# Two-layer trunk on one core: five blocks per MLP with four Strassen groups, twelve raw tiles, the norm scale applied at the down projection

## The chip, the cores and the metric

The kernel runs on one core of a Trainium2 chip. The metric is the device time of one execution in microseconds (us), lower is better. TensorE (PE) multiplies matrices, VectorE (DVE) and ScalarE (ACT) work elementwise, GpSimd (POOL) hardly takes part, and SyncE (SP) issues the transfers of the weights.

## What is computed

256 tokens of 2048 channels pass through two layers: a mixer, then an MLP with a squared ReLU, both behind an RMS norm and added to the residual stream. The change touches the two MLPs and, by the order of work, the pooling mixer of layer 1 that stands between them.

```python
D_FF = 4 * D_MODEL                       # 8192

def rms_norm(x, g):
    y = xf * lax.rsqrt(jnp.mean(xf * xf, axis=-1, keepdims=True) + EPS)
    return y * g

def multiscale_pool(h, w, b, scale):     # group i: trailing mean over WINDOWS[i] minus the token
    ...
    y = jnp.einsum('btgc,gcd->btgd', d, w).reshape(bsz, t, D_MODEL) + b
    return y * scale

def sq_relu_mlp(h, w_up, w_down):
    u = jax.nn.relu(h @ w_up)
    return (u * u) @ w_down

for layer in range(DEPTH):               # layer 0: hybrid mixer, layer 1: multiscale_pool
    x = x + mix
    x = x + sq_relu_mlp(rms_norm(x, mlp_norm[layer]), mlp_w_up[layer], mlp_w_down[layer])
```

The norm's factor r of a token can be taken out of the MLP: (relu(r·h W))² = r² (relu(h W))², since r is positive.

## The kernel before

**Precision.** Each fp32 operand is split in two parts: hi, a rounded copy (ACT, L235), and lo, the rest (DVE, L236: raw − hi). A product is made of three matmuls, hi·hi, hi·lo and lo·hi.

**Steps.** All weights are streamed in 846 *steps*, mostly of 512 KB. SP issues the load of a step into a *raw* tile (L206), ACT and DVE split it into a hi and a lo tile (L235, L236), PE multiplies. There are 7 raw tiles and 4 tiles each of hi and lo, used in turn; a load waits until its raw tile's last reader, the lo of seven steps before, is done. Loads are written 9 steps ahead of their matmuls (`AHEAD_LOAD`), splits 3 (`AHEAD_SPLIT`).

**Units.** Steps belong to units of one kind each. *up*: 256 columns of w_up over 16 k-tiles (a k-tile is 128 rows), in a transposed form, with pairs of a 512-wide (L963) and a 256-wide (L965) matmul. *down*: 512 columns of w_down, two k-tiles and 12 matmuls a step (L971), evacuated into the residual `x_sb` by L834; the last chunk of the kernel is cut into two units of 256 columns. *Strassen group*: 1024 columns of w_up in a form of Strassen's algorithm, with fewer products; 12 *sa* steps and 16 *sb* steps of 6 matmuls each (L734). The sb steps come in pairs, and before a pair is split, DVE replaces its two raw tiles by differences in place (L222 to L225). When a group is done, `gen_s` combines the results, squares them and transposes them into the block data.

**Blocks.** The 8192 inner channels of an MLP are taken in 4 blocks of 2048: first the block's up units, then its down units, which multiply the block's 16 k-tiles of u² by 512 columns of w_down at a time, in 8 steps for each of 4 chunks. Block 0 consists of 8 up units; blocks 1 to 3 of 4 up units and one Strassen group. The steps of the next block's Strassen group are held back and let in between the down steps of the block before, as `due()` says: the 12 sa steps beside the first 10 or so of the 32 down steps, then the 8 pairs of sb steps.

**Norm.** The factor r of the norm is spread to a row by a small matmul (`spread`, L317) and multiplied in at the up units' evacuation (L874) and in `gen_s`.

**Pool.** With the first MLP's last down units, `finish` loads the pool's data into slots whose old contents have been read: the pool matrix into slot 6 (L843, copied to slot 7 by ACT in L845), bias into slot 4 and scale into slot 5 (L850). DVE multiplies bias by scale (L854) and adds the product to the residual (`add_bias`, L765). Slots 4 to 7 held the last block's u², k-tiles 0 to 3, 4 to 7 and so on. The pool units' results are split (L863 on ACT, L864 on DVE), multiplied by window matrices (L776 to L780) and added to the residual.

**Order.** The program is written step by step; generators (`lane`) put the other work between the steps. A scheduler then orders each engine's instructions; SP and DVE work their queues in that order.

Of the kernel before, what the change touches and what calls it, by code (L numbers as in the profile page):

```python
# [16 lines left out]
P = 128  # L17
# [5 lines left out]
DFF = 8192  # L23
FB = 2048
NB = DFF // FB
WINS = (2, 4, 8, 16)
# [14 lines left out]
X_EARLY = ((0, 14), (1, 2), (1, 6), (1, 10))  # L41
RAWS, AHEAD_LOAD = 7, 9
WARM = 2
# [4 lines left out]
def plan():  # L48
# [9 lines left out]

    def unit(w, r0, nk, c0, n, kind, arg, src, k0=0, turned=False):
        units.append(dict(w=w, r0=r0, nk=nk, c0=c0, n=n, kind=kind, arg=arg, src=src, k0=k0,  # L60
                          turned=turned))

# [13 lines left out]
    for layer in range(2):  # L76
        if layer == 1:
            for g in range(4):
                unit("pool_w", 512 * g, 4, 0, 512, "pool", g, "pool", 4 * g)
        for b in range(NB):  # L80
            for i in range(8 if b == 0 else 4):
                unit("w_up", D * layer, KT, b * FB + 256 * i, 256, "up", (layer, b, i),
                     f"mlp{layer}", turned=True)
            if b + 1 < NB:
                for kind in ("sa", "sb"):
                    unit("w_up", D * layer, KT, (b + 1) * FB + FB // 2, 512, kind,
                         (layer, b + 1), f"mlp{layer}")
# [12 lines left out]
    for u, d in enumerate(units):  # L100
        c0, n = d["c0"], d["n"]
        if d["kind"] == "sa":
            tiles = [t for k in range(0, KT, 2) for t in ((k, c0), (k + 1, c0), (k + 1, c0 + n))]
            held += [[(u, j, tiles[j : j + 2])] for j in range(0, len(tiles), 2)]
            at = 0
        elif d["kind"] == "sb":
            for k in range(0, KT, 2):
                held.append([(u, 2 * k, [(k, c0), (k, c0 + n)]),
                             (u, 2 * k + 2, [(k + 1, c0 + n), (k + 1, c0)])])
        else:  # L110
            ks = list(range(0, d["nk"], 4 if d["turned"] else 2))
            if u == 0:
                ks = [0, 1, 2, 3] + ks[2:]
            for j, (k, e) in enumerate(zip(ks, ks[1:] + [d["nk"]])):
                seq.append((u, k, [(kk, c0) for kk in range(k, e)]))
                if d["kind"] == "down":
                    at += 1
                    while held and at >= due(20 - len(held)):
                        seq += held.pop(0)
    assert not held  # L120
    steps, off = [], 0
    for u, k, tiles in seq:
        steps.append((u, k, tiles, off))
        off += len(tiles) * P * units[u]["n"]
    return units, steps


@with_exitstack
def tile_trunk(ctx: ExitStack, tc: tile.TileContext, x_in, xt_in, w_all, prm_in,
# [21 lines left out]
    def t4(n, dt=F32):  # L151
        return new("t4", [P, 1036], dt, bufs=5)[:, :n]

# [28 lines left out]
    def load_x(q):  # L182

        m, c = q // 2, slice(D // 2 * (q % 2), D // 2 * (q % 2) + D // 2)
        if q == 0:
# [7 lines left out]
               "u0": u_blk[0], "u1": u_blk[1]}  # L193
    units, steps = plan()
    raws, splits = {}, {}
    done = {"load": 0, "split": 0}

    def load(i):
        u, k, tiles, off = steps[i]
        n, nk = units[u]["n"], len(tiles)  # L200
        raw = v3(new("raw", [P, 1024], bufs=RAWS)[:, : nk * n], nk, n)
        if u == 0:
# [123 lines left out]

    def row2(name):
        return rs[name, "row"][:, None, :].to_broadcast([P, 2, T])

    def norm_chunk(name, c, tiles, slot0, gain):  # L330
# [19 lines left out]

# [328 lines left out]
    def gen_u(b, i, ea, eb, base):  # L679
        yield  # L680
        act.activation(eb, ea, AF.Square)
        if i % 2 == 0:
# [110 lines left out]
    def finish(u, ps):  # L793
# [36 lines left out]
        elif kind in ("out", "down"):  # L830
            c = arg if kind == "out" else arg[2]
            cs = slice(d["c0"], d["c0"] + d["n"])
            for m in range(MT):
                dve.tensor_tensor(x_sb[m][:, cs], x_sb[m][:, cs], ps[:, m, : d["n"]], ALU.add)  # L834
# [32 lines left out]
        elif kind == "up":  # L867
            layer, b, i = arg
            name = f"mlp{layer}"
            need(lambda: (name, "row") in rs)  # L870
            e = ev()
            ea, eb = v3(e[:, 0], 2, T), v3(e[:, 1], 2, T)
            add_halves(ea, ps)
            dve.scalar_tensor_tensor(ea, ea, 0.0, row2(name), ALU.max, ALU.mult)  # L874
            lane.append(gen_u(b, i, ea, eb, u_base(layer, b)))
# [53 lines left out]
    for i, (u, k, tiles, _) in enumerate(steps):  # L929
# [118 lines left out]
```

## Time and profile before

| | us |
|---|---|
| three runs: median (lowest to highest) | 2166.05 (2165.43 to 2166.27) |
| profiled execution, its own time | 2164.82 |
| its span | 2163.0 |
| ACT busy | 1203.2 |
| DVE busy with lo (L236), 846 instructions | 1012.2 |
| DVE busy with the sb operations (L222 to L225), 48 of each | 132.2 |

Rows of the timeline give the start in us, the duration in us, engine, line, operation, output<-inputs, and in brackets the idle time before it with what ended it. Busy times of PE are modelled at a matmul's end, so consecutive matmuls overlap and the distance of their starts tells more. A wait in the list of waits names who waited, for whom, the sum in us, how many times, and the longest.

### The profile page before, as it was taken

To read this page: it belongs to the slowest core of one execution; us is meant where nothing else is said; L and a number is where in the kernel's file an instruction comes from. 1 tells how busy PE (TensorE), PEld (TensorE's weight loads), DVE (VectorE), ACT (ScalarE), POOL (GpSimd) and SP (SyncE) were. 2 spreads that over 40 slices of the span, in tenths; PEclk is the share of its full clock that TensorE was granted. 3 is DMA by queue.
4 is the path that set the end of the run, shared out by engine and by line. 5 is a ranking of instruction groups with operands and counts; after the bars stand their busy time and mean duration, and the time that the engine had idled before them with its cause. 6 is when DMAs were issued, how large, how long until landed. Compare 5 with 4: busy or idle time off the path is not lost.

```text
span 2163.0 us, 28389 instructions
## 1 busy us (share of the span) xinstructions
PE 2154.4 (100%) x10613; PEld 1820.6 (84%) x10613; DVE 1541.7 (71%) x1908; ACT 1203.2 (56%) x1401; POOL 21.7 (1%) x21
## 2 busy tenths in 40 slices
PE   9999999999999999999999999999999999999999
PEld 8888888888888888888888888878888888888888
DVE  6988766656545586876886886578778678678754
ACT  7665456665644465555555555456555555555543
POOL 0000000000000000000000000000000000000000
PEclk9999999999999999999999999999999999999999
DMA  9665455555665567777776776565677677677663
GB/s 334 204 204 166 159 184 166 175 166 166 207 192 191 170 197 240 245 232 215 248 247 202 246 253 186 187 224 162 197 257 250 194 245 243 214 247 238 224 204 117
DMA packets 129002, 454.32 MB, mean 210 GB/s; under 512 B 14496, under 2 KB 17248, under 8 KB 128608
## 3 DMA queue, kind: packets, MB, share of 16 engines
q1 hardware_dynamic: 128000, 451.36, 64.4%
q8 instruction: 83, 1.36, 0.3%
q10 hardware_dynamic: 864, 1.15, 0.2%
q14 instruction: 55, 0.45, 0.1%
HBM read 450.32 MB, written 2.13 MB: 209 GB/s over the span
## 4 chain that ended last, share of the span: by engine, by line
PE 97%; DVE 1%; DMA 1%; issue 0%; ACT 0%; SPq 0%; DVEq 0%; ACTq 0%
PE acc L971 58%; PE acc L963 16%; PE bg L734 10%; PE acc L965 9%; PE bg L294 1%; PE bg L522 1%; DVE lo L236 0%; DMA raw<-w_all 0%; PE bg L579 0%; PE bg L669 0%; PE bg L614 0%; DMA st<-prow_in 0%; DVE st L765 0%; PE bg L610 0%; PE bg L671 0%
## 5 line engine op out<-in xcount | busy, mean ns | idle before, releaser
L235 ACT ACTIVATE hi<-raw 128x1024 fp32r<-128x1024 f32 (+2 forms) x846 | 887.6, 1049 | 889.8 <-PE acc L971 586.2
L236 DVE TENSOR_TENSOR lo<-raw,hi 128x1024 fp32r<-128x1024 f32 (+2 forms) x846 | 1012.2, 1206 | 454.7 <-ACT hi L235 432.4
L971 PE MATMUL acc<-hi,st 128*128 128x512 f32 (+2 forms) x3840 | 1165.6, 386 | 0.9 <-ACT hi L235 0.9
L971 PEld LDWEIGHTS acc<-hi,st 128*128 128x128 f32 x3840 | 710.9, 188 | 142.1 <-ACT hi L235 2.4
L971 PE MATMUL acc<-lo,st 128*128 128x512 f32 (+2 forms) x1920 | 736.2, 385 | 0.4 <-DVE lo L236 0.3
L963 PE MATMUL acc<-st,hi 128*128 128x512 f32 x1568 | 552.4, 394 | 0.0
L965 PE MATMUL acc<-st,lo 128*128 128x256 f32 x1568 | 441.8, 282 | 0.0
L971 PEld LDWEIGHTS acc<-lo,st 128*128 128x128 f32 x1920 | 360.6, 188 | 74.1 <-DVE lo L236 2.2
L963 PEld LDWEIGHTS acc<-st,hi 128*128 128x128 f32 x1568 | 294.3, 188 | 62.1 <-issue 1.4
L965 PEld LDWEIGHTS acc<-st,lo 128*128 128x128 f32 x1568 | 296.3, 189 | 2.0 <-issue 1.4
L734 PE MATMUL bg<-hi,st 128*128 128x512 f32 x672 | 206.9, 389 | 0.0
L734 PEld LDWEIGHTS bg<-hi,st 128*128 128x128 f32 x672 | 126.1, 188 | 26.3
L734 PE MATMUL bg<-lo,st 128*128 128x512 f32 x336 | 130.7, 389 | 0.0
L734 PEld LDWEIGHTS bg<-lo,st 128*128 128x128 f32 x336 | 63.1, 188 | 13.0
L834 DVE TENSOR_TENSOR st<-st,acc 128x512 f32<-128x512 f32 (+1 forms) x74 | 46.4, 669 | 15.9 <-PE acc L971 15.6
L222 DVE TENSOR_TENSOR raw<-raw 128x512 f32<-128x512 f32 x48 | 33.1, 689 | 31.1 <-DMA raw<-w_all 31.0
L223 DVE TENSOR_TENSOR raw<-raw,raw 128x512 f32<-128x512 f32 x48 | 33.1, 690 | 20.7 <-DMA raw<-w_all 19.9
L282 ACT ACTIVATE st<-bg,prm 128x256 fp32r<-128x256 f32 x64 | 28.4, 467 | 22.5 <-DVE st L283 20.9
L325 DVE TENSOR_TENSOR ev<-acc,ev 128x512 f32<-128x512 f32 x40 | 27.4, 686 | 11.6 <-ACT ev L324 11.6
L283 DVE SCALAR_TENSOR_TENSOR st<-bg,prm,st 128x256 fp32r<-128x256 f32 x64 | 29.5, 481 | 8.2 <-ACT st L282 8.2
L225 DVE TENSOR_TENSOR raw<-raw 128x512 f32<-128x512 f32 x48 | 33.1, 690 | 1.0
L224 DVE TENSOR_TENSOR raw<-raw,raw 128x512 f32<-128x512 f32 x48 | 32.9, 686 | 0.2
(187 smaller groups left out, 949.7 us busy)
## 6 DMA issues: line engine op xcount, KB each, us to landing
raw<-w_all SPq DMA_DIRECT2D x818, 512.0 KB, 3.8
raw<-w_all SPq DMA_DIRECT2D x20, 256.0 KB, 2.8
st<-x_in SPq DMA_DIRECT2D x8, 512.0 KB, 7.8
st<-scr SPq DMA_DIRECT2D x8, 512.0 KB, 6.1
raw<-w_all SPq DMA_DIRECT2D x8, 288.0 KB, 8.1
st<-prow_in SPq DMA_DIRECT2D x2, 1024.0 KB, 6.3
st<-xt_in SPq DMA_DIRECT2D x6, 256.0 KB, 7.4
st<-pmat_in SPq DMA_DIRECT2D x1, 768.0 KB, 6.2
```

The lines of the kernel that those rows point to most:

```text
L222: dve.tensor_tensor(raw[:, 0], raw[:, 1], raw[:, 0], ALU.subtract)
L223: dve.tensor_tensor(raw[:, 1], two[:, 0], raw[:, 1], ALU.subtract)
L224: dve.tensor_tensor(two[:, 0], two[:, 0], raw[:, 0], ALU.subtract)
L225: dve.tensor_tensor(two[:, 1], two[:, 0], two[:, 1], ALU.subtract)
L235: act.activation(hi, raw, AF.Copy)
L236: dve.tensor_tensor(lo, raw, hi.bitcast(F32), ALU.subtract)
L283: dve.scalar_tensor_tensor(dst[:, 1, c], ps, gain, dst[:, 0, c].bitcast(F32), ALU.mult, ALU.subtract)
L734: pe.matmul(sps[q], st[h], w[:, j], start=p == 0 and w is hi and h == 0, stop=p == KT // 2 - 1 and w is lo)
L834: dve.tensor_tensor(x_sb[m][:, cs], x_sb[m][:, cs], ps[:, m, : d["n"]], ALU.add)
L963: pe.matmul(ps[:, f].rearrange("p (h t) -> p h t", h=2), hi[:, kk, fs], t[:, :, c], start=first, stop=False)
L965: pe.matmul(ps[:, f, :T], lo[:, kk, fs], t[:, 0, c], start=False, stop=last)
L971: pe.matmul(ps[:, m, :n], t[:, h % 2, c, m * P : (m + 1) * P], (hi, hi, lo)[h][:, kk], start=first and h == 0, stop=last and h == 2)
```

## The change

Each MLP is cut into five blocks: 2048 columns in 8 up units, then four blocks of 1536, each of 2 up units (512 columns) and a Strassen group (1024). So a layer has four Strassen groups instead of three. Down units of blocks 1 to 4 have 12 k-tiles and 6 steps per chunk; their k-tiles are taken in the order 4 to 11, then 0 to 3, which puts the Strassen group's first. `due()` is scaled to the number of down steps.

Outside the mixers, loads may also go to the 5 tiles of the scratch ring `t4`, in a fixed alternation with the 7 raw tiles (`homes`): twelve raw tiles there. `AHEAD_LOAD` is 14.

r is no longer spread to a row for the MLPs. The up results get a plain ReLU on ACT and the square; r² (a column per token half) is multiplied in where a down unit is evacuated, now a SCALAR_TENSOR_TENSOR (x + r²·y).

Lines shift: lo is L270, hi L269, the sb operations L256 to L259, the load L240, the down evacuation L875, bias times scale L895, `add_bias` L800, the pool matmuls' split L904 and L905, the loads of prow L891 and of pmat L884, `put_hi_lo` L318 (L283 before).

```diff
-FB = 2048
-NB = DFF // FB
+SW = 1024
+BLOCKS = ((2048, 0), (512, SW), (512, SW), (512, SW), (512, SW))
+NB = len(BLOCKS)
+BASE = [sum(map(sum, BLOCKS[:b])) for b in range(NB)]
...
-RAWS, AHEAD_LOAD = 7, 9
+RAWS, SPARE, AHEAD_LOAD = 7, 5, 14
...
-            for i in range(8 if b == 0 else 4):
+            for i in range(BLOCKS[b][0] // 256):
...
-                    unit("w_down", DFF * layer + b * FB, KT, c0, n, "down", (layer, b, c),
-                         f"u{b % 2}")
-
-    def due(i):
-        return 1 + 10 * i // 12 if i < 12 else 13 + 19 * (i - 12) // 8
+                    unit("w_down", DFF * layer + BASE[b], sum(BLOCKS[b]) // P, c0, n, "down",
+                         (layer, b, c),
+                         f"u{b % 2}",
+                         own=BLOCKS[b][0] // P if b else 0)
+
+    def due(i, n):
+        a = 5 * n // 16
+        return 1 + a * i // 12 if i < 12 else a + 3 + (n - a - 3) * (i - 12) // 8
...
+        kts = [*range(own, nk), *range(own)]
...
+def homes(units, steps):
+    def free(d):
+        if d["kind"] not in ("up", "sa", "sb", "down"):
+            return False
+        layer, b = d["arg"][:2]
+        return not ((layer, b) == (0, NB - 1) and d["kind"] == "down"
+                    or (layer, b) == (1, 0) and d["kind"] == "up" and d["arg"][2] < 6)
+
+    rings, at, res = {"raw": [], "t4": []}, 0, []
+    size = {"raw": RAWS, "t4": SPARE}
+    for i, (u, *_) in enumerate(steps):
+        ring = "raw"
+        if free(units[u]):
+            at = (at + 1) % (RAWS + SPARE)
+            ring = "t4" if at * SPARE % (RAWS + SPARE) < SPARE else "raw"
+        r = rings[ring]
+        res.append((ring, r[-size[ring]] if len(r) >= size[ring] else -1))
+        r.append(i)
+    return res
...
-        while done["load"] < min(len(steps), i + 1 + AHEAD_LOAD):
+        while (done["load"] < min(len(steps), i + 1 + AHEAD_LOAD)
+               and home[done["load"]][1] < done["split"]):
...
+            if name != "pool":
+                rs[name, "sq"] = new("rsq", [P, MT], bufs=2)
+                dve.tensor_tensor(rs[name, "sq"], r, r, ALU.mult)
...
-        if c == 3 and name != "pool":
-            yield from spread(name)
...
+        act.activation(ea, ea, AF.Relu)
         act.activation(eb, ea, AF.Square)
...
-        act.activation(a[:, 0:2], a[:, 0:2], AF.Relu, scale=r[:, 0:1])
+        act.activation(a[:, 0:2], a[:, 0:2], AF.Relu)
...
-                dve.tensor_tensor(x_sb[m][:, cs], x_sb[m][:, cs], ps[:, m, : d["n"]], ALU.add)
+                o, y = x_sb[m][:, cs], ps[:, m, : d["n"]]
+                if kind == "out":
+                    dve.tensor_tensor(o, o, y, ALU.add)
+                else:
+                    dve.scalar_tensor_tensor(o, y, r2[:, m : m + 1], o, ALU.mult, ALU.add)
...
-            dve.scalar_tensor_tensor(ea, ea, 0.0, row2(name), ALU.max, ALU.mult)
```

**DVE, in the sb steps beside block 0's down units.** The rows are the instructions of DVE's queue, output<-inputs. Names are tiles with running numbers; a raw or t4 tile is written by a load, and the one that takes its buffer over is the seventh raw tile after it before the change, and after it the seventh raw or the fifth t4 tile. Before, `raw_1487` takes over the buffer of `raw_1465`, which `lo_1486` reads last:

```order
L236 TENSOR_TENSOR lo_1486_8670<-raw_1465_8568,hi_1485_8669 128x1024
L224 TENSOR_TENSOR raw_1477_8629<-raw_1477_8629,raw_1474_8611 128x512
L225 TENSOR_TENSOR raw_1477_8629<-raw_1477_8629 128x512
L236 TENSOR_TENSOR lo_1489_8688<-raw_1468_8580,hi_1488_8687 128x1024
L222 TENSOR_TENSOR raw_1487_8685<-raw_1487_8685 128x512
```

After, `t4_1284` takes over the buffer of `t4_1244`, which `lo_1283` reads last:

```order
L270 TENSOR_TENSOR lo_1283_7497<-t4_1244_7313,hi_1282_7496 128x1024
L270 TENSOR_TENSOR lo_1286_7515<-raw_1249_7327,hi_1285_7514 128x1024
L256 TENSOR_TENSOR t4_1284_7512<-t4_1284_7512 128x512
L270 TENSOR_TENSOR lo_1289_7533<-raw_1254_7345,hi_1288_7532 128x1024
L270 TENSOR_TENSOR lo_1292_7549<-t4_1257_7363,hi_1291_7548 128x1024
L257 TENSOR_TENSOR t4_1284_7512<-raw_1287_7530,t4_1284_7512 128x512
L270 TENSOR_TENSOR lo_1295_7561<-raw_1260_7381,hi_1294_7560 128x1024
L258 TENSOR_TENSOR raw_1287_7530<-raw_1287_7530,t4_1284_7512 128x512
L259 TENSOR_TENSOR raw_1287_7530<-raw_1287_7530 128x512
```

Before, a lo and two sb operations stand between the lo that frees the buffer and the first operation on its new tile; here, after the change, one lo.

**DVE, from the first MLP's last down unit to the pool units.** Before (`st4` and `st5` are bias and scale, `st12` and `st13` the residual, `acc_72` the last down unit's result):

```order
L236 TENSOR_TENSOR lo_2016_11720<-raw_1992_11582,hi_2015_11719 128x1024
L854 TENSOR_TENSOR st4_1936_11251<-st4_1936_11251,st5_1937_11252 128x512
L854 TENSOR_TENSOR st4_1936_11251<-st4_1936_11251,st5_1937_11252 128x512 x3
L765 TENSOR_TENSOR st12_849_4939<-st12_849_4939,st4_1936_11251 128x512
...
L236 TENSOR_TENSOR lo_2019_11738<-raw_1995_11602,hi_2018_11737 128x1024
L236 TENSOR_TENSOR lo_2022_11756<-raw_1999_11624,hi_2021_11755 128x1024
L834 TENSOR_TENSOR st12_849_4939<-st12_849_4939,acc_72_11608 128x512
L834 TENSOR_TENSOR st13_850_4940<-st13_850_4940,acc_72_11608 128x512
```

After (`acc_74` is the last down unit's result, `acc_75` the first pool unit's):

```order
L875 SCALAR_TENSOR_TENSOR st13_850_4940<-acc_74_11684,rsq_1044_6082,st13_850_4940 128x512
L270 TENSOR_TENSOR lo_2068_11816<-raw_2044_11678,hi_2067_11815 128x1024
L270 TENSOR_TENSOR lo_2078_11863<-raw_2048_11700,hi_2077_11862 128x1024
L372 TENSOR_REDUCE sum_2070_11835<-ss_2002_11426 128x2
...
L895 TENSOR_TENSOR st4_1997_11399<-st4_1997_11399,st5_1998_11400 128x512
L895 TENSOR_TENSOR st4_1997_11399<-st4_1997_11399,st5_1998_11400 128x512 x3
L800 TENSOR_TENSOR st12_849_4939<-st12_849_4939,st4_1997_11399 128x512
...
L905 SCALAR_TENSOR_TENSOR t4_2080_11881<-acc_75_11819,rstd_2071_11837,t4_2079_11880 128x512
L270 TENSOR_TENSOR lo_2083_11889<-raw_2051_11718,hi_2082_11888 128x1024
```

The multiplication of bias by scale and the six additions that follow stood ahead of the last down unit's evacuation; they now stand behind it, and ahead of the first pool unit's L905.

**SP, at the same place.** Before:

```order
L206 DMA raw_2002_11642<-w_all 128x1024
L850 DMA st4_1936_11251<-prow_in 128x2048
L206 DMA raw_2007_11670<-w_all 128x1024
L206 DMA raw_2011_11697<-w_all 128x1024
L850 DMA st5_1937_11252<-prow_in 128x2048
L206 DMA raw_2014_11717<-w_all 128x1024
L843 DMA st6_1933_11245<-pmat_in 128x1536
```

After:

```order
L891 DMA st5_1998_11400<-prow_in 128x2048
L240 DMA raw_2056_11746<-w_all 128x1024
L240 DMA raw_2060_11773<-w_all 128x1024
L884 DMA st6_1994_11393<-pmat_in 128x1536
L240 DMA raw_2063_11793<-w_all 128x1024
L240 DMA raw_2066_11813<-w_all 128x1024
L891 DMA st4_1997_11399<-prow_in 128x2048
```

The load of the bias into slot 4 was the first of the three and is now the last; slot 4's old contents, the k-tiles 0 to 3 of the last block, are read last.

More of the change, by code (lines that the diff above doesn't have):

```diff
@@ L57, in plan, with unit @@
     units = []
-    def unit(w, r0, nk, c0, n, kind, arg, src, k0=0, turned=False):
+    def unit(w, r0, nk, c0, n, kind, arg, src, k0=0, turned=False, own=0):
+        kts = [*range(own, nk), *range(own)]
         units.append(dict(w=w, r0=r0, nk=nk, c0=c0, n=n, kind=kind, arg=arg, src=src, k0=k0,
-                          turned=turned))
+                          turned=turned, kts=kts))
     unit("w_in", 0, KT, CB, 512, "b", None, "h")
@@ L80, in plan @@
         for b in range(NB):
-            for i in range(8 if b == 0 else 4):
-                unit("w_up", D * layer, KT, b * FB + 256 * i, 256, "up", (layer, b, i),
+            for i in range(BLOCKS[b][0] // 256):
+                unit("w_up", D * layer, KT, BASE[b] + 256 * i, 256, "up", (layer, b, i),
                      f"mlp{layer}", turned=True)
-            if b + 1 < NB:
+            if b + 1 < NB and BLOCKS[b + 1][1]:
                 for kind in ("sa", "sb"):
-                    unit("w_up", D * layer, KT, (b + 1) * FB + FB // 2, 512, kind,
+                    unit("w_up", D * layer, KT, BASE[b + 1] + BLOCKS[b + 1][0], 512, kind,
                          (layer, b + 1), f"mlp{layer}")
@@ L114, in plan @@
             for j, (k, e) in enumerate(zip(ks, ks[1:] + [d["nk"]])):
-                seq.append((u, k, [(kk, c0) for kk in range(k, e)]))
+                seq.append((u, k, [(kk, c0) for kk in d["kts"][k:e]]))
                 if d["kind"] == "down":
                     at += 1
-                    while held and at >= due(20 - len(held)):
+                    while held and at >= due(20 - len(held), 2 * d["nk"]):
                         seq += held.pop(0)
@@ L151, in t4 @@
     def t4(n, dt=F32):
-        return new("t4", [P, 1036], dt, bufs=5)[:, :n]
+        return new("t4", [P, 1036], dt, bufs=SPARE)[:, :n]
     def bank():
@@ L194, in tile_trunk @@
     units, steps = plan()
+    home = homes(units, steps)
     raws, splits = {}, {}
@@ L200, in load @@
         n, nk = units[u]["n"], len(tiles)
-        raw = v3(new("raw", [P, 1024], bufs=RAWS)[:, : nk * n], nk, n)
+        raw = (t4(nk * n) if home[i][0] == "t4" else
+               new("raw", [P, 1024], bufs=RAWS)[:, : nk * n])
+        raw = v3(raw, nk, n)
         if u == 0:
@@ L325, in add_halves @@
         dve.tensor_tensor(dst, ps[:, :, :T], dst, ALU.add)
-    def row2(name):
-        return rs[name, "row"][:, None, :].to_broadcast([P, 2, T])
     def norm_chunk(name, c, tiles, slot0, gain):
@@ L377, in turned @@
         add_halves(xT[:, :, 3:], ps)
-        dve.tensor_tensor(xT[:, :, 3:], xT[:, :, 3:], row2("hyb"), ALU.mult)
+        dve.tensor_tensor(xT[:, :, 3:], xT[:, :, 3:], rs["hyb", "row"][:, None, :].to_broadcast([P, 2, T]), ALU.mult)
         return xT
@@ L737, in gen_s @@
     def gen_s(layer, b, base):
-        a, r = sev["a"], rs[f"mlp{layer}"]
+        a = sev["a"]
         p4, p5, p6, p7 = (sps.pop(q) for q in (4, 5, 6, 7))
@@ L751, in gen_s @@
         yield
-        act.activation(e, e, AF.Relu, scale=r[:, 1:2])
+        act.activation(e, e, AF.Relu)
         act.activation(e, e, AF.Square)
@@ L757, in gen_s @@
         for q in range(2):
-            yield from to_ring(lambda m: (a, e)[m][:, q], u_blk[b % 2], 8 + 4 * q,
-                               slot(base + 2 + q), None)
+            yield from to_ring(lambda m: (a, e)[m][:, q], u_blk[b % 2],
+                               BLOCKS[b][0] // P + 4 * q, slot(base + BLOCKS[b][0] // 512 + q),
+                               None)
     pl = {}
@@ L832, in finish @@
             cs = slice(d["c0"], d["c0"] + d["n"])
+            r2 = rs[f"mlp{arg[0]}", "sq"] if kind == "down" else None
             for m in range(MT):
-                dve.tensor_tensor(x_sb[m][:, cs], x_sb[m][:, cs], ps[:, m, : d["n"]], ALU.add)
+                o, y = x_sb[m][:, cs], ps[:, m, : d["n"]]
[3 more added lines that the diff above has]
+                    dve.scalar_tensor_tensor(o, y, r2[:, m : m + 1], o, ALU.mult, ALU.add)
                 if kind == "down" and arg[:2] == (1, NB - 1):
@@ L868, in finish @@
             layer, b, i = arg
-            name = f"mlp{layer}"
-            need(lambda: (name, "row") in rs)
             e = ev()
@@ L945, in tile_trunk @@
                 b = d["arg"][1]
-                need(lambda: b == 0 or len(u_blk[(b - 1) % 2]) == 16)
-                for kk in range(KT):
-                    u_blk[b % 2].pop(kk, None)
+                need(lambda: b == 0 or len(u_blk[(b - 1) % 2]) == sum(BLOCKS[b - 1]) // P)
+                u_blk[b % 2].clear()
         ps = accs[u]
@@ L955, in tile_trunk @@
                 load_x(q)
-        need(lambda: all(k0 + k + kk in src for kk in range(n2)))
+        need(lambda: all(k0 + kt in src for kt, _ in tiles))
         for kk in range(n2):
-            t, c = src[k0 + k + kk]
+            t, c = src[k0 + tiles[kk][0]]
             first, last = k + kk == 0, k + kk == nk - 1
```

## The prediction

> **What bounds the kernel now.** I read the busy shares first, then the chain of work that ended last, then the windows of one MLP block.
>
> ```profile
> span 2163.0 us, 28389 instructions
> PE 2154.4 (100%) x10613; PEld 1820.6 (84%) x10613; DVE 1541.7 (71%) x1908; ACT 1203.2 (56%) x1401; POOL 21.7 (1%) x21
> PE 97%; DVE 1%; DMA 1%; issue 0%; ACT 0%; SPq 0%; DVEq 0%; ACTq 0%
> L971 PE MATMUL acc<-lo,st 128*128 128x512 f32 (+2 forms) x1920 | 736.2, 385 | 0.4 <-DVE lo L236 0.3
> core 0: us, PE busy (x) PEld busy (x) DVE busy (x) ACT busy (x) POOL busy (x), PEclk, DMA share, GB/s
> 872.00:938.00 66.00, 66.00 (x293) 54.66 (x292) 57.17 (x65) 33.95 (x33) 0.00 (x0) 1.00 0.73 244
> 950.00:996.00 46.00, 46.00 (x269) 40.75 (x268) 30.65 (x34) 26.62 (x32) 0.00 (x0) 1.00 0.61 190
> ```
>
> PE is 97% of the chain and waited 0.3 us for a lo tile in 1920 such matmuls. So a matmul taken away shortens the kernel, as long as nothing else becomes late. The two windows show where that is near: from 872 to 938, where down steps alternate with sb steps (I call this a **stretch**; there are six), DVE is busy 57.17 of 66.00 us. From 950 to 996, in up units, it is 30.65 of 46. The granted clock is 1.00 in both.
>
> **1. Matmuls, on the path.** From the timeline of PE (start, duration, line, number of instructions):
>
> ```profile
> 852.27 0.62 PE L734 MATMUL bg<-hi,st 128*128 128x512 f32 x2
> 852.95 0.62 PE L734 MATMUL bg<-hi,st 128*128 128x512 f32 x2
> 819.81 0.39 PE L963 MATMUL acc<-st,hi 128*128 128x512 f32 x1
> 827.44 0.39 PE L963 MATMUL acc<-st,hi 128*128 128x512 f32 x1
> 961.25 0.27 PE L294 MATMUL bg<-cst,att_b 128*128 128x128 f32 x1
> 961.60 0.48 PE L963 MATMUL acc<-st,hi 128*128 128x512 f32 x1
> 961.92 0.28 PE L965 MATMUL acc<-st,lo 128*128 128x256 f32 x1
> ```
>
> Start to start, three 512-wide matmuls take 852.95 − 852.27 = 0.68 us, so 0.227 each. A down step (12 of them) is then 2.72 us and a Strassen step (6) is 1.36. Between 819.81 and 827.44 lie 22 pairs of one 512-wide and one 256-wide matmul: 7.63 / 22 = 0.347 a pair. A Strassen group covers 1024 columns with (12 + 16) × 6 = 168 matmuls, where four up units take 4 × 2 × 16 = 128 pairs. The change makes one group more in each layer: −256 pairs × 0.347 = −88.8, and +336 × 0.2267 = +76.2. Each group also brings 16 transposes in four bursts more: a burst moves the next L965 from 961.48 (0.23 after 961.25) to 961.92, so 0.44, and 8 bursts cost +3.5. The spread of r to a row goes, which is four 128-wide matmuls in L317 for each MLP; at the price of a burst of four transposes (estimate) −0.9. **Sum −10.0.** No engine but PE works on these, so all of it is on the path.
>
> The Trainium skill, "TensorE: Matmul & The Clock Gate", section "Back-to-back issue gap", gives N/2.4 + 2.5 ns for an isolated warm matmul: 216 and 109 ns, and the exchange would be −256 × 0.325 + 336 × 0.216 = −10.6 instead of −12.6. The rows say 227 and 347, so I keep them.
>
> **2. The stretches, where DVE decides.** DVE must subtract hi for each step (L236) and, for each pair of sb steps, do four operations in place (L222 to L225). Timelines of DVE and PE, the landing times of the loads issued from 872 to 938, and two rows of the list of waits (us in total, times, longest):
>
> ```profile
> 871.51 2.35 DVE L236 TENSOR_TENSOR lo<-raw,hi 128x1024 fp32r<-128x1024 f32 x2
> ...
> 875.19 1.22 DVE L236 TENSOR_TENSOR lo<-raw,hi 128x1024 fp32r<-128x1024 f32 x1
> 876.32 0.68 DVE L224 TENSOR_TENSOR raw<-raw,raw 128x512 f32<-128x512 f32 x1
> 877.04 0.69 DVE L225 TENSOR_TENSOR raw<-raw 128x512 f32<-128x512 f32 x1
> 877.87 1.23 DVE L236 TENSOR_TENSOR lo<-raw,hi 128x1024 fp32r<-128x1024 f32 x1
> 879.97 0.69 DVE L222 TENSOR_TENSOR raw<-raw 128x512 f32<-128x512 f32 x1 [0.88 <-DMA raw<-w_all]
> 879.93 0.39 PE L734 MATMUL bg<-lo,st 128*128 128x512 f32 x1
> 1280.09 0.50 PE L971 MATMUL acc<-lo,st 128*128 128x512 f32 x1 [0.30 <-DVE lo L236]
> 925.18 1.28 DVE L834 TENSOR_TENSOR st<-st,acc 128x512 f32<-128x512 f32 x2
> DMA to landing us min/median/max: 3.4/4.4/5.0
> DVE raw L222 <- DMA raw<-w_all: 31.0, 23, 3.2
> DVE raw L223 <- DMA raw<-w_all: 19.9, 25, 2.8
> ```
>
> A lo costs 1.13 us (875.19 to 876.32), an sb operation 0.61 to 0.72, a pair of evacuations 1.28. DVE enters the stretch 6.07 us ahead: the lo that PE reads at 879.93 ended at 873.86. What eats this lead is the head of DVE's queue. L222 at 879.97 needs a tile whose load could start only when the lo at 875.19 had freed its buffer; it waited 0.88 us for the DMA and all the lo's behind it waited too. These waits are 31.0 + 19.9 = 50.9 us in the kernel, 8.5 in a stretch. The lead lasted, but only just: at 1280.09 PE already waited 0.30 us.
>
> After the change DVE has the same four operations per pair in less matmul time. Six of the eight stretches lie beside down units of 24 steps: from first to last pair 16 × 1.36 + 12 × 2.72 = 54.4 us of PE against 28 × 1.13 + 32 × 0.66 + 2 × 1.4 = 55.6 of DVE (before: 65.3 against about 60). Twelve raw tiles instead of seven must then take away the waits, or the lead goes. How far an sb operation stands behind the lo that frees its buffer is in DVE's order. I walked that order, with these durations, SP starting a load when the freeing lo ends, and landings that the views allow: 3.5 us for a load alone, up to 4.6 with another one under way. On the kernel before the walk gives 9.0 us of waits in a stretch (8.5 in the trace) and a lowest lead of 0.9 (in the trace stretches come down to 0). After, the 24-step stretches have waits of 3.7 us and a lowest lead of 0.6. The two 32-step stretches beside block 0 come out worse than before: in four of eight pairs the L222 operation (now L256) stands only one or two lo's and up to two sb operations behind the lo that frees its buffer, 1.1 to 2.4 us for a landing of 3.5 to 4.6, the waits sum to 12.5 us, and PE stalls 2.5 us. With 4.4 us for every load, the median of that window, the walk gives 16 us of stalls over all eight; with 3.5 for every load none; with 5.0, 51 (and 23 before, which the trace excludes). I take **+5** for the two long stretches and **+1.5** for the six short ones, since the trace has lower leads than the walk. Bounds 0 and 16.
>
> By the Trainium skill, "DMA: Bandwidth & Descriptors", section "Anatomy of one DMA — SWDGE (gpsimd) path", a transfer takes 2.0 us plus its bytes at 436 GB/s, which is 3.2 us for 512 KB at any time, for another path of issue than SP's. The trace's 3.4 to 5.0 disagrees for loads that overlap; by the rule this term would be 0.
>
> **3. From the first MLP to the pool units.** Before, bias and scale are loaded and multiplied under the last down steps (the view of L850's DMAs, then the timelines).
>
> ```profile
> L850 SPq DMA_DIRECT2D st<-prow_in x2: 327/328/328, 1415.1 to 1421.0; - x2
> DMA to landing us min/median/max: 6.0/6.3/6.7
> 1427.71 2.50 DVE L854 TENSOR_TENSOR st<-st,st 128x512 f32<-128x512 f32 x4 [1.34 <-DMA st<-prow_in]
> 1430.13 3.70 DVE L765 TENSOR_TENSOR st<-st,st 128x512 f32<-128x512 f32 x6
> 1432.19 0.61 PE L971 MATMUL acc<-hi,st 128*128 128x512 f32 x2
> 1433.26 1.49 ACT L845 ACTIVATE st<-st 128x1536 fp32r<-128x1536 f32 x1
> 1445.48 0.68 PE L780 MATMUL bg<-t,st 128*128 128x512 f32 x2
> 1445.99 0.62 PE L971 MATMUL acc<-hi,st 128*128 128x512 f32 x2
> ```
>
> The last down unit's matmuls end and the first pool unit's begin at 1432.19 (t0), and the first group's window matmuls end at 1445.99, t0 + 13.8. The bias sits in the slot that holds block data k 0 to 3. These are now read last, so SP issues the bias last of the three, at about t0 + 0.2, and it lands 6.0 to 6.7 later. In DVE's new order L895 × 4 and the additions (2.42 + 3.6 = 6.0 us) stand behind the evacuation, two lo's and norm operations, and ahead of L905, which the window matmuls need. The pool matrix's copy on ACT (1.49) comes ahead of the first of these lo's hi, which then starts near t0 + 3.6; the second follows a step, 2.72, later at 6.3 and ends at 7.4, and with the norm operations DVE reaches L895 at about t0 + 7.9. The six additions end at 13.9; then come a norm operation (0.5), two more additions (1.2), L905, a lo and L905 again (0.75 + 1.1 + 0.75), until 18.2. The window matmuls end near t0 + 18.4. **+4.6**, between 0 (other work fills it) and +6.0 (all of it exposed). By the DMA rule above the bias would be there earlier, but DVE arrives after it anyway, and the term stays.
>
> **4. What costs nothing.** The evacuation with r² (L834 to L875) becomes a SCALAR_TENSOR_TENSOR from PSUM and L874 goes. Groups of instructions by line (count, then busy us, mean ns of one, idle time before):
>
> ```profile
> L864 DVE SCALAR_TENSOR_TENSOR t<-acc,rstd,t 128x512 fp32r<-128x512 f32 x8 | 6.0, 747 | 0.0
> L834 DVE TENSOR_TENSOR st<-st,acc 128x512 f32<-128x512 f32 x70 | 44.9, 683 | 11.2 <-PE acc L971 10.9
> L874 DVE SCALAR_TENSOR_TENSOR ev<-ev,rrow 128x512 f32<-128x512 f32 x40 | 27.6, 690 | 1.0
> L681 ACT ACTIVATE ev<-ev 128x512 f32<-128x512 f32 x40 | 25.0, 624 | 2.1 <-DVE ev L874 2.1
> ```
>
> 74 × 0.06 more and 40 × 0.69 less for DVE; 32 Relus of about 0.62 for ACT, in up units, where the 950 to 996 window leaves each a third of its time. Without that cover it would be 20 us of ACT. Gained DVE time there is worth nothing either, since PE does not wait. The k order of down units is free: their first tiles come from the Strassen group, whose transposes end in the up units before.
>
> **Sum:** −10.0 + 5 + 1.5 + 4.6 = **+1.1**. The profiled run of before took 2164.82 us (span 2163.0), 1.2 under the median of its runs, 2166.05; so 2165.9 there and **2167.2** beside the median.
>
> **Rivals.** Differences up to 0.2%, 4.3 us, can't be told from none: faster is below 2161.7, slower above 2170.4.
> (a) *The stretches hold*: loads land at 3.5 as those alone do, PE never waits. −10.0 + 4.6 = −5.4, 2160.7; with the additions hidden too, 2156.1. For it: the walk's six short stretches keep a lead. Against it: the median 4.4. This is also what the skill's DMA rule gives. Chance 0.25.
> (b) *DVE becomes the wall in the stretches*: loads take 4.4, each sb operation holds the queue, 16 us of stalls: −10.0 + 16 + 4.6 = +10.6, 2176.7. It decides from 9.7 us of stalls on, 1.2 a stretch (4.3 + 10.0 − 4.6). For it: the lead of 0 at 1280.09, and DVE's 55.6 against 54.4. Against: waits in the short stretches halved by the walk. Chance 0.28.
> (c) *The change doesn't do what it says*: the spare tiles come no sooner than the seven did, and a short stretch has the old 8.5 us of waits: 55.6 + 8.5 − 54.4 − 6.1 = 3.6 us × 6 = 22, so 2166.05 − 10.0 + 22 + 5 + 4.6 = 2187.7. Chance 0.05.
> The forecast has 0.42. Faster 0.25, same 0.42, slower 0.33. The range, 2156 to 2180, takes in both ends of (a) and (b)'s price with some play, and leaves out (c). The forecast's own range is 2162 to 2170.
>
> **What would show it.** Right: PE's busy time about 10 us lower; stalls of PE on lo in the stretches of block 0 with L256 waiting 2 us and more for the DMA, few in the others; the window matmuls ending about 18 us after the last down matmul. Wrong: no wait of PE for lo (a), or waits in every stretch (b). A granted clock below 1.00 would upset term 1, and landings over 5 us term 2.

## The result: about the same, with ten microseconds won on PE and given back in two places

The changed kernel takes 2170.41 us (median of 13 runs, 2165.55 to 2176.70), the kernel before 2165.66 (13 runs, 2164.00 to 2167.49). The ratio is 1.0025, with a 95% interval of 1.0016 to 1.0035: 4.7 us slower where +1.1 was forecast. The difference is small, but clear of the noise. The runs of the changed kernel lie over 11 us, those of before over 3.5; the profiled one, from which the figures below are, took 2168.91, 1.5 under its median and 4.1 above the profiled run of before.

From the page of the changed kernel: its span, busy times, the shares of the chain by engine; then two groups, the matmuls that read a lo tile; then rows of the list of waits.

```profile
span 2167.0 us, 28186 instructions
PE 2149.7 (99%) x10437; PEld 1805.7 (83%) x10437; DVE 1594.2 (74%) x1972; ACT 1240.8 (57%) x1451; POOL 21.7 (1%) x21
PE 90%; DVE 4%; DMA 4%; issue 1%; ACT 0%; SPq 0%; DVEq 0%; ACTq 0%
L1008 PE MATMUL acc<-lo,st 128*128 128x512 f32 (+2 forms) x1912 | 736.0, 386 | 3.3 <-DVE lo L270 3.2
L768 PE MATMUL bg<-lo,st 128*128 128x512 f32 x448 | 174.9, 390 | 2.2 <-DVE lo L270 2.0
DVE raw L256 <- DMA raw<-w_all: 28.7, 29, 3.3
DVE t L256 <- DMA t<-w_all: 20.8, 18, 3.3
PE bg L811 <- DVE t L905: 3.2, 1, 3.2
```

PE's share of the chain has fallen from 97% to 90%; DVE and DMA have come in with 4% each. PE now waits 5.2 us for lo tiles where it waited 0.3; the loss by distance of starts, below, is larger, since the end of the matmul before a stop is modelled and covers part of it. The first sb operation of a pair (L256) waits 49.5 us for the DMA where it waited 31.0. The second (L257) waits 8.6 where it waited 19.9, so the waits of both are 58.1 us in eight stretches, 7.3 in each, after 50.9 in six, 8.5 in each: less for a pair of steps, but there is less matmul time beside it. By part, from the first matmul of a part to its last (or to the next part's first) in the timelines, and with the time lost in the stretches, which is their length, from the first sb matmul to the last, less their matmuls at 0.2268 us each:

| us | before | after | difference |
|---|---|---|---|
| mixer of layer 0, to the first up matmul | 737.4 | 737.8 | +0.4 |
| first MLP | 694.5 | 694.0 | −0.5 |
| from its last matmul to the second MLP's first | 29.7 | 35.0 | +5.3 |
| second MLP | 697.2 | 696.2 | −1.0 |
| of the two MLPs, lost in the stretches | 0.9 (6) | 9.8 (8) | +8.9 |

The MLPs without the stretches' losses are 10.3 us shorter. So three terms make the result: −10.3, +8.9 and +5.3. PE's busy time fell by only 4.7 us, where the prediction looked for 10: part of the stops, and matmuls that ran slowly (the last section), count as busy.

**A stretch.** Timelines of DVE and of PE, in the one beside block 0 of layer 0:

```profile
907.24 1.22 DVE L270 TENSOR_TENSOR lo<-raw,hi 128x1024 fp32r<-128x1024 f32 x1
911.76 0.69 DVE L256 TENSOR_TENSOR t<-t 128x512 f32<-128x512 f32 x1 [3.31 <-DMA t<-w_all]
912.37 1.22 DVE L270 TENSOR_TENSOR lo<-raw,hi 128x1024 fp32r<-128x1024 f32 x1
911.89 0.61 PE L1008 MATMUL acc<-hi,st 128*128 128x512 f32 x2
913.65 0.50 PE L1008 MATMUL acc<-lo,st 128*128 128x512 f32 x1 [1.14 <-DVE lo L270]
DMA to landing us min/median/max: 3.3/4.2/5.4
```

This is the place of the first order shown above: L256 on `t4_1284` stands one lo behind the one that frees its buffer, waits 3.31 us for the load, and the lo behind it ends at 913.59, when PE has stood for 1.14 us. At the 13 longest stops in the stretches (7.5 of the 9.8 us) the next matmul reads a lo tile, and in the 20 us before each of them DVE stood idle for loads alone, never for a hi tile of ACT. The landing row is that of the loads issued from 872 to 945; 4.4 was the median before.

**From the first MLP to the pool.** Timelines of DVE and PE, and the view of the loads of bias and scale:

```profile
L891 SPq DMA_DIRECT2D st<-prow_in x2: 328/328/328, 1420.4 to 1432.2; - x2
1439.20 2.49 DVE L895 TENSOR_TENSOR st<-st,st 128x512 f32<-128x512 f32 x4
1441.60 3.70 DVE L800 TENSOR_TENSOR st<-st,st 128x512 f32<-128x512 f32 x6
1446.81 0.75 DVE L905 SCALAR_TENSOR_TENSOR t<-acc,rstd,t 128x512 fp32r<-128x512 f32 x1
1447.61 0.50 PE L811 MATMUL bg<-t,st 128*128 128x512 f32 x1 [3.16 <-DVE t L905]
1449.40 0.79 PE L815 MATMUL bg<-t,st 128*128 128x512 f32 x1 [0.57 <-DVE t L905]
1449.99 1.05 PE L1008 MATMUL acc<-hi,st 128*128 128x512 f32 x2
```

The last down unit ends at 1432.05. The bias is issued at 1432.2, DVE's ten operations run from 1439.20 to 1445.30, and PE stands 3.16 and 0.57 us for L905. The window matmuls end at 1449.99, 17.9 us after the last down unit (13.8 before).

### The profile page after: what moved, and what is told of

Its sections match the earlier page's. It is cut to its first block, busy times and chain, and to the rows that moved or that the text cites. A ratio compares the mean times of both kernels' runs of the same rounds, so it can differ in the third digit from the quotient of the medians.

```text
span 2167.0 us, 28186 instructions
## 1 busy us (share of the span) xinstructions
PE 2149.7 (99%) x10437; PEld 1805.7 (83%) x10437; DVE 1594.2 (74%) x1972; ACT 1240.8 (57%) x1451; POOL 21.7 (1%) x21
## 4 chain that ended last, share of the span: by engine, by line
PE 90%; DVE 4%; DMA 4%; issue 1%; ACT 0%; SPq 0%; DVEq 0%; ACTq 0%
PE acc L1008 53%; PE acc L1000 14%; PE bg L768 12%; PE acc L1002 7%; DVE lo L270 3%; DMA raw<-w_all 2%; DMA t<-w_all 2%; PE bg L329 1%; PE bg L555 1%; PE bg L612 0%; PE bg L702 0%; PE bg L647 0%; ACT hi L269 0%; DVE st L800 0%; DVE t L257 0%
## 5 line engine op out<-in xcount | busy, mean ns | idle before, releaser
L269 ACT ACTIVATE hi<-raw 128x1024 fp32r<-128x1024 f32 (+2 forms) x633 | 664.5, 1050 | 613.6 <-PE acc L1008 431.7
L270 DVE TENSOR_TENSOR lo<-raw,hi 128x1024 fp32r<-128x1024 f32 (+2 forms) x633 | 760.3, 1207 | 315.5 <-ACT hi L269 303.2
L1000 PE MATMUL acc<-st,hi 128*128 128x512 f32 x1312 | 464.7, 396 | 0.0
L269 ACT ACTIVATE hi<-t 128x1024 fp32r<-128x1024 f32 (+1 forms) x235 | 247.3, 1052 | 232.2 <-PE acc L1008 150.9
L1002 PE MATMUL acc<-st,lo 128*128 128x256 f32 x1312 | 369.1, 282 | 0.0
L270 DVE TENSOR_TENSOR lo<-t,hi 128x1024 fp32r<-128x1024 f32 (+1 forms) x235 | 284.4, 1210 | 83.5 <-ACT hi L269 80.8
L1000 PEld LDWEIGHTS acc<-st,hi 128*128 128x128 f32 x1312 | 246.3, 188 | 51.6 <-issue 1.4
L768 PE MATMUL bg<-hi,st 128*128 128x512 f32 x896 | 275.9, 389 | 0.0
L1002 PEld LDWEIGHTS acc<-st,lo 128*128 128x128 f32 x1312 | 247.9, 189 | 2.1 <-issue 1.4
L875 DVE SCALAR_TENSOR_TENSOR st<-acc,rsq,st 128x512 f32<-128x512 f32 (+1 forms) x82 | 57.1, 732 | 10.4 <-PE acc L1008 10.2
L256 DVE TENSOR_TENSOR raw<-raw 128x512 f32<-128x512 f32 x40 | 27.6, 691 | 28.7 <-DMA raw<-w_all 28.7
L318 DVE SCALAR_TENSOR_TENSOR st<-bg,prm,st 128x256 fp32r<-128x256 f32 x64 | 29.8, 480 | 7.8 <-ACT st L317 7.6
L256 DVE TENSOR_TENSOR t<-t 128x512 f32<-128x512 f32 x24 | 16.6, 691 | 20.8 <-DMA t<-w_all 20.8
```

The lines of the kernel that those rows point to most:

```text
L256: dve.tensor_tensor(raw[:, 0], raw[:, 1], raw[:, 0], ALU.subtract)
L269: act.activation(hi, raw, AF.Copy)
L270: dve.tensor_tensor(lo, raw, hi.bitcast(F32), ALU.subtract)
L318: dve.scalar_tensor_tensor(dst[:, 1, c], ps, gain, dst[:, 0, c].bitcast(F32), ALU.mult, ALU.subtract)
L768: pe.matmul(sps[q], st[h], w[:, j], start=p == 0 and w is hi and h == 0, stop=p == KT // 2 - 1 and w is lo)
L875: dve.scalar_tensor_tensor(o, y, r2[:, m : m + 1], o, ALU.mult, ALU.add)
```

## Experiments

Each run's kernel was timed against the kernel before on the same chip; the ratio's 95% interval stands behind it. "Lost" is the time lost in the stretches of its profiled run, as in the table above. The kernel before took 2165.2 to 2166.0 (medians) beside them, so a difference to the changed kernel's 2170.41 is good to about 1 us.

**1. No sb operations.** Is it DVE's queue at all?

```diff
-            two = raws[i + 1]
-            dve.tensor_tensor(raw[:, 0], raw[:, 1], raw[:, 0], ALU.subtract)
-            dve.tensor_tensor(raw[:, 1], two[:, 0], raw[:, 1], ALU.subtract)
-            dve.tensor_tensor(two[:, 0], two[:, 0], raw[:, 0], ALU.subtract)
-            dve.tensor_tensor(two[:, 1], two[:, 0], two[:, 1], ALU.subtract)
+            pass
```

> The changed kernel without the four DVE operations of each sb pair (the Strassen weights are then not differenced, so that part of the computation is left out). Theory A, PE's stalls in the stretches come from these operations in DVE's queue: the 9.8 us of stalls go, 2170.4 becomes about 2161. Rival B, the stretches are slow because loads or hi tiles come late: 2169 to 2171, and PE still waits for hi or lo there.

2160.02 us, ratio 0.9973 (0.9962 to 0.9983). Nothing is lost in any stretch, and the two MLPs take 688.8 and 691.4 us. The groups of matmuls that read lo:

```profile
L1004 PE MATMUL acc<-lo,st 128*128 128x512 f32 (+2 forms) x1912 | 735.4, 386 | 0.1
L764 PE MATMUL bg<-lo,st 128*128 128x512 f32 x448 | 174.3, 389 | 0.0
```

Theory A holds, and B falls: with the loads as they were, the waits are gone. The hi tiles of the sb steps no longer come behind the differences either, but at the stops above DVE had waited for no hi tile.

**2. sb operations that wait for nothing, first try.** Run 1 takes away both DVE's work and the wait; which of them matters?

```diff
-            two = raws[i + 1]
-            dve.tensor_tensor(raw[:, 0], raw[:, 1], raw[:, 0], ALU.subtract)
...
+            for _ in range(4):
+                dve.tensor_tensor(dum, dum, dum, ALU.subtract)
```

> The same four DVE operations per pair, but on one scratch tile (496 instead of 512 wide), so that none of them waits for a load (the weights' differences are left out). Theory A1, it is the wait for the DMA at the head of DVE's queue: stalls go as without the operations, 2161 to 2163. Rival A2, it is the amount of DVE's work, 55.6 us in 54.4 us of a short stretch: most stalls stay, 2167 to 2170.

2171.19 us, ratio 1.0025 (1.0016 to 1.0035), which looks like A2, and isn't. The view of the scratch operations' line:

```profile
L256 DVE TENSOR_TENSOR dum<-dum x256: 610/672/678, 1.8 to 560.5; 128x496 f32<-128x496 f32 x128
```

Operations that depend on nothing were ordered ahead: all ran before 561 us, in the mixer, which grew from 737.8 to 749.5 us. The stretches had none. The run tells nothing between A1 and A2; it was made again as run 9.

**3. Other slots for the pool's data.**

```diff
-                    pl["mat"] = slot(7, (P, 12, P))
+                    pl["mat"] = slot(4, (P, 12, P))
-                    pl["bias"], pl["scale"] = (slot(4 + i, (P, D), F32) for i in range(2))
+                    pl["bias"], pl["scale"] = (slot(i, (P, D), F32) for i in (5, 7))
```

> The changed kernel with other slots for the pool's data: scale in slot 7, which is free, bias in slot 5, read before slot 4, the pool matrix copied to slot 4. Theory: the 5.2 us lost between the first MLP and the second come from the bias that lands after the last down unit, so 2170.4 becomes about 2165 and L895 starts before the last down unit ends. Rival: DVE's order or ACT's copy holds the window matmuls anyway: 2169 to 2171.

2165.14 us, ratio 0.9998 (0.9989 to 1.0007): 5.3 us less than the changed kernel's 2170.41. The part between the MLPs takes 29.1 us instead of 35.0; the stretches lose 10.1 as ever. DVE's and PE's timelines:

```profile
1427.72 2.50 DVE L895 TENSOR_TENSOR st<-st,st 128x512 f32<-128x512 f32 x4
1430.13 2.49 DVE L800 TENSOR_TENSOR st<-st,st 128x512 f32<-128x512 f32 x4
1445.90 0.63 PE L815 MATMUL bg<-t,st 128*128 128x512 f32 x2
1446.37 0.40 PE L1008 MATMUL acc<-hi,st 128*128 128x512 f32 x1
```

The last down unit ends at 1433.2, and L895 now starts 5.5 us ahead of that; the window matmuls end 13.2 us behind it. So the slots were the whole of the loss there. The run moves three buffers at once; that the bias is the one that matters rests on the view above, where it was issued at 1432.2, behind the last down unit, while scale had been issued at 1420.4.

**4. Seven raw tiles.**

```diff
     def free(d):
-        if d["kind"] not in ("up", "sa", "sb", "down"):
-            return False
+        return False
```

> The changed kernel with the seven raw tiles alone (no load goes to a t4 tile). If the twelve tiles shorten the waits of the sb operations: stalls rise by 7 to 8 us by a walk along DVE's order, about 2178. Rival, the spare tiles do nothing: 2170.

2177.94 us, ratio 1.0053 (1.0041 to 1.0066). Lost: 18.7 us, about 3 in each short stretch; the two long ones lose 0 and 0.7. So the spare tiles are worth 7.5 us over all, rival (c) of the prediction falls, and in the two long stretches they do harm: 4.3 us lost with them in the changed kernel, 2.7 in run 3 (one profiled run each).

**5. The sb pairs spread wider.**

```diff
-        a = 5 * n // 16
-        return 1 + a * i // 12 if i < 12 else a + 3 + (n - a - 3) * (i - 12) // 8
+        a = 3 * n // 16
+        return 1 + a * i // 12 if i < 12 else a + 2 + (n - a - 2) * (i - 12) // 8
```

> The changed kernel with due() altered: the sa steps go beside the first 3/16 of a block's down steps instead of 5/16, and the sb pairs start two down steps later instead of three, so they are spread over 16 to 24 down steps instead of 14 to 19. If the stretches stall because an sb operation stands too near behind the lo that frees its buffer, each pair then has more matmul time: stalls fall from 9.8 us to 0 to 3, 2170.4 becomes 2161 to 2164. Rival, the stalls come from single landings over 4.5 us whatever the distance: 2168 to 2171.

2162.60 us, ratio 0.9989 (0.9980 to 0.9998). Lost: 0.8 us, nearly all in one stretch. A further 1.8 us are lost outside what the table counts, in the sa steps ahead of the first sb matmul, beside which DVE now does the first sb pairs; 1.7 of them in one place. The operations still wait for the DMA; DVE's timeline, and PE's at that place:

```profile
904.18 1.22 DVE L270 TENSOR_TENSOR lo<-raw,hi 128x1024 fp32r<-128x1024 f32 x1
907.25 0.69 DVE L256 TENSOR_TENSOR raw<-raw 128x512 f32<-128x512 f32 x1 [1.85 <-DMA raw<-w_all]
1245.14 0.69 DVE L256 TENSOR_TENSOR raw<-raw 128x512 f32<-128x512 f32 x1 [1.60 <-DMA raw<-w_all]
1254.68 0.69 DVE L256 TENSOR_TENSOR t<-t 128x512 f32<-128x512 f32 x1 [1.23 <-DMA t<-w_all]
1260.89 0.50 PE L1008 MATMUL acc<-lo,st 128*128 128x512 f32 x1 [1.30 <-DVE lo L270]
```

With more matmul time per pair most such waits, like the one at 907.25, are made good again. The rival, that single late landings stall PE whatever the spacing, falls; what is left, 2.6 us, comes behind the same waits, most of it where DVE does the first pairs among the sa steps.

**6. Both.** Runs 3 and 5 together.

> Both the spread sb pairs and the other slots for the pool's data. If the two losses are separate they add up: 2170.4 - 5.3 - 7 to 10 = 2155 to 2158, below the kernel before. Rival, they share a cause or DVE's order changes with both: 2161 to 2166.

2156.63 us, ratio 0.9962 (0.9949 to 0.9974): the two losses add, and this version is faster than both kernels. In its profiled run 3.4 us were lost in the two long stretches and none in the six short ones, another 1.8 in the sa steps ahead of two short ones, and the part between the MLPs took 29.7.

**7. The k-tiles of the down units in natural order.**

```diff
-                         own=BLOCKS[b][0] // P if b else 0)
+                         own=0)
```

> The changed kernel with the down units' k-tiles in natural order again (0 to 11). Slot 4 is then free first, so the bias comes early and the pool part loses its 5.3 us; but the first down step of each block needs the tiles that the last up unit has just made, at 8 places 0 to 2 us each. Together 2165 to 2181; if the hand-over costs nothing, 2165. Rival for the pool: it stays at 35 us though the bias is early.

2183.15 us, ratio 1.0083 (1.0069 to 1.0097), at the far end of what was expected. The part between the MLPs stays at 35.6 us, as the rival said. Timelines of DVE and PE there, and PE's at the last block's hand-over from up to down units:

```profile
1442.50 2.50 DVE L895 TENSOR_TENSOR st<-st,st 128x512 f32<-128x512 f32 x4 [1.25 <-DMA st<-prow_in]
1444.91 3.69 DVE L800 TENSOR_TENSOR st<-st,st 128x512 f32<-128x512 f32 x6
1448.53 0.74 DVE L875 SCALAR_TENSOR_TENSOR st<-acc,rsq,st 128x512 f32<-128x512 f32 x1
1449.32 1.54 PE L329 MATMUL bg<-cst,st 128*128 128x128 f32 x6 [3.17 <-DVE st L875]
1372.82 0.54 PE L1008 MATMUL acc<-hi,st 128*128 128x512 f32 x1 [2.76 <-ACT st L314]
1374.57 1.05 PE L1008 MATMUL acc<-hi,st 128*128 128x512 f32 x2
```

The bias is early, but scale, in slot 5, is issued at 1434.6, 5.7 us ahead of the end of the last down unit, since a unit of 6 steps is 16 us long and not 22. L895 then waits in DVE's queue between the two evacuations (L875) and PE stands behind the second. In the last block of each layer PE stands for the tiles of the last up unit, which the natural order needs early: 3.4 us at 1369.7 to 1373.6, then matmuls 0.427 us apart, some 5 us together, and the same at 2112.5 in layer 1. The stretches lose 14.4, 4.6 more than in the changed kernel, and the sa steps ahead of them 1.4 more. Of the 18.3 us between the two spans (2185.3 and 2167.0), the two hand-overs make about 10, these 6, the part between the MLPs 0.5 and the mixer 1.4; why the stretches and the mixer lose more here is left open. The order that takes the Strassen k-tiles first thus pays for itself, at these hand-overs.

**8. The norm scale alone, on the kernel before.**

```diff
-                dve.tensor_tensor(x_sb[m][:, cs], x_sb[m][:, cs], ps[:, m, : d["n"]], ALU.add)
+                    dve.scalar_tensor_tensor(o, y, r2[:, m : m + 1], o, ALU.mult, ALU.add)
...
-            dve.scalar_tensor_tensor(ea, ea, 0.0, row2(name), ALU.max, ALU.mult)
...
-            yield from spread(name)
```

> The kernel before with the norm scale alone changed: no spread of r to a row, plain Relu, r squared multiplied at the down units' evacuation. By the prediction's step 4 it costs nothing and saves the spread's matmuls: 2164.5 to 2166. Rival, the longer evacuation and the extra Relu delay lo and hi tiles in the stretches: 2167 to 2170.

2166.01 us, ratio 1.0000 (0.9991 to 1.0009). No difference that can be measured. In its profiled run the stretches lost 2.9 us (0.9 before), but that run was the slowest of its eleven. A small price of the longer evacuation, made up for by the spread's matmuls, is not excluded.

**9. Work without the wait.** Two operations on a scratch tile in each sb step, which read the lo of the step before.

```diff
+        if units[u]["kind"] == "sb":
+            old = splits[i - 1][1][:, 0, :496].bitcast(F32)
+            for _ in range(2):
+                dve.tensor_tensor(dum, old, old, ALU.subtract)
```

> The run before this with scratch operations did not tell: they depended on nothing, so all 256 ran before 561 us, in the mixer, and the stretches had none. Here each pair of sb steps has four DVE operations (496 wide, into one scratch tile) that read the lo tile of the step before, so they stand in the stretches, cost DVE about 0.6 us each and wait for no load (the weights' differences are left out). Theory A1, the waits for the DMA at the head of DVE's queue make the stalls: no stalls in the stretches, 2160 to 2163. Rival A2, the amount of DVE's work does: stalls of 5 us and more, 2166 to 2170.

2159.37 us, ratio 0.9973 (0.9962 to 0.9984). Nothing is lost in any stretch; the MLPs take 688.8 and 691.4 us, as without the operations. The second stretch in this run, and the second and third of the changed kernel, in the windows (PE, PEld, DVE, ACT, POOL busy, clock, DMA share, GB/s):

```profile
1021.00:1078.00 57.00, 57.00 (x253) 47.18 (x252) 53.95 (x63) 30.71 (x30) 0.00 (x0) 1.00 0.80 258
1020.00:1077.00 57.00, 56.59 (x250) 46.37 (x249) 49.16 (x56) 30.24 (x29) 0.00 (x0) 1.00 0.76 262
1148.00:1206.00 58.00, 56.84 (x249) 46.16 (x248) 48.72 (x54) 30.08 (x29) 0.00 (x0) 1.00 0.77 253
```

With the work alone DVE is busier in these 57 us, 53.95, and PE never stands; in the changed kernel DVE is busy 49.16 and PE stands. A1 holds, A2 falls: the amount of work alone costs nothing; what costs is the wait at the head of DVE's queue on top of it, where too little matmul time is left to make it good (run 5).

## Why the prediction was right, and where it was short

**The mechanisms were right; two sizes were short.** The forecast 2167.2 is 3.2 us under the measured time. That 2170.41 lies inside 2156 to 2180 says little, since this range is 24 us wide; the forecast's own range, 2162 to 2170, is missed by 0.4, and the kernel stands on the line of 2170.4 from which it was to count as slower. The sum of its terms stands against the profiled runs like this:

| term | forecast | measured |
|---|---|---|
| 1, matmuls | −10.0 | −10.3 to −10.6 (experiment 1: 1380.2 us for both MLPs without losses, before 1391.7 with 0.9) |
| 2, two long stretches | +5 | +4.3 (2.0 and 2.3) |
| 2, six short stretches | +1.5 | +5.5 (0.0 to 2.0) |
| lost in the stretches of before, not in the sum | 0 | −0.9 |
| 3, first MLP to pool | +4.6 | +5.3 |

**1. Matmuls.** The exchange held, and run 1 shows it without the rest.

**2. The stretches** are where the forecast was too small. The walk along DVE's order got the place and the size of the long ones: waits of 11.6 and 11.8 us where it had 12.5, stalls of 2.0 and 2.3 where it had 2.5. In the short ones it had waits of 3.7 us; the trace has 4.8 to 6.7, 5.8 on average, so the waits were cut by a third from the 8.5 of before, and not by more than half. For the lowest lead of 0.6 us that the walk left there, the prediction added 1.5 us over all six, on the ground that the trace of before shows lower leads than the walk. That ground asked for more: where the walk had 0.9 for each stretch of before, the trace has 1.3, 0.9, 0.1, 0.1, 0.1 and 0.8, so a lead of 0.6 in the walk is none, and in the trace of after every short stretch comes down to about 0.1. The mis-sized term is this 1.5, which measured 5.5. It is also the part that varies: two of the six lost 0.0 and 0.3, two over 1.2, in one run, and the changed kernel's runs spread over 11 us, those of experiment 9 over 1.7. So the sign to look for, few stalls outside the two long stretches, did not come true. The mechanism is that of the prediction, shown by runs 1 and 9 together; landings took up to 5.4 us, over the 5 that it had named as upsetting this term. What the prediction put beside it, DVE's 55.6 us of work in 54.4, decides nothing by itself: run 9 has that work and no stall.

The Trainium skill's fit ("DMA: Bandwidth & Descriptors", "Anatomy of one DMA — SWDGE (gpsimd) path": 2.0 us and the bytes at 436 GB/s, for another path of issue than SP's) gives an estimate of 3.2 us for 512 KB and would have made this term 0. The trace has 3.3 to 5.4, median 4.2, and the stalls; here the measurement decides against using it.

**3. The pool** came as worked out: L895 at t0 + 7.2 (forecast 7.9), the window matmuls' end at t0 + 17.9 (18.4). That end came 4.1 us later than before, and 1.2 us more went to something that the term left out, the slow matmuls told of below: 5.3 in all, not 4.6. Run 3 shows the cause, by taking it away. The prediction's view that the k order alone moved the bias is half of it: run 7 has the old order and no gain, because the shorter units leave less time for the loads in either order.

**4. What costs nothing** is borne out by run 8 to the accuracy of a measurement. The count there was short: the kernel after has 82 evacuations with r² (L875) where the MLPs before had 66 (L834 without the mixer's 8), about 12 us of DVE that the step left out. Runs 1 and 9 have them too and lose nothing in the stretches.

**The rivals.** (a), stretches that hold, would need landings of 3.5 us; only the kernel with the sb pairs spread came near it (run 5, 2162.60). (b), DVE as the wall with 16 us of stalls, overstated the same mechanism; the 9.8 measured are just at the 9.7 from which it was to decide. (c) falls with run 4: without the spare tiles 18.7 us are lost.

## What to carry to other kernels

Here an operation of DVE that waited for a load held everything behind it (3.31 us at one L256), so what counts is not only how busy the engine is but how much of its queue stands between the event that lets the load start and the operation that needs it; read that from the order, price it with landing times of loads that overlap, and treat a lead below the scatter of the old trace as none. When a stage is shortened, look at what was hidden beside it: here shorter down units left the loads of the next stage without cover, and other buffers for them brought 5.3 us back. If a probe operation is to cost time at one place, tie it to data of that place, and check in the trace that it ran there.

## What the runs showed of the hardware

After PE had stood for 3.16 us and run again for a moment, its clock was halved for a while. The windows of the changed kernel, from before the stop to after it:

```profile
1440.00:1444.00 4.00, 4.00 (x19) 3.34 (x18) 4.00 (x7) 2.02 (x4) 0.00 (x0) 1.00 0.30 122
1444.00:1448.00 4.00, 0.84 (x4) 0.32 (x3) 4.00 (x8) 1.27 (x2) 0.00 (x0) 1.00 0.00 0
1450.00:1452.00 2.00, 2.00 (x6) 1.61 (x5) 2.00 (x4) 0.00 (x0) 0.00 (x0) 0.50 0.88 264
1452.00:1456.00 4.00, 4.00 (x18) 3.26 (x18) 3.15 (x4) 2.10 (x4) 0.00 (x0) 0.95 0.49 140
```

The granted clock is 0.50 from 1450 to 1452; the five matmuls from 1449.99 start 0.427 us apart instead of 0.227, the next 0.375, so 1.2 us go on top of the 3.7 that PE stood. The clock stood at 0.50 from 1449.0 to 1452.4, 3.4 us. In experiment 1 the stop was shorter and the slow matmuls more, twelve: the clock stood at 0.50 from 1444.2 to 1451.0, 6.8 us. Its timeline and windows:

```profile
1443.10 0.50 PE L807 MATMUL bg<-t,st 128*128 128x512 f32 x1 [2.50 <-DVE t L901]
1444.89 0.80 PE L811 MATMUL bg<-t,st 128*128 128x512 f32 x1 [0.56 <-DVE t L901]
1445.00:1447.00 2.00, 2.00 (x5) 1.61 (x6) 2.00 (x3) 0.00 (x0) 0.00 (x0) 0.50 0.92 252
1449.00:1451.00 2.00, 2.00 (x6) 1.55 (x5) 0.63 (x1) 0.53 (x1) 0.00 (x0) 0.50 0.37 102
```

The Trainium skill has this ("TensorE: Matmul & The Clock Gate", "Why this matters for your kernels": no idle gaps of PE over about 3 us); the trace agrees in kind, and shows it for a gap of 2.5 us too, which another of 0.56 us followed. The length of the stop alone does not set the moment: in the changed kernel the clock fell 1.4 us after PE had resumed, in experiment 7, at 1448.2, while PE had stood for 2.1 us and was still standing. The stalls of 1.1 us in the stretches left the clock at 1.00 (the windows of experiment 9 above).
